# A hybrid decoder layer on one core: token blocks of 256, 512, 256 with the middle one dense, and its first expert products queued through the last block

## The chip, the core and the metric

The kernel runs on one core of a Trainium2 chip. The metric is the device time of one execution in microseconds (us); lower is better. The engines are PE (TensorE matmul, with PEld for its weight loads), DVE (VectorE), ACT (ScalarE), POOL (GpSimd) and SP (SyncE, which issues most DMAs). Each engine works through its own queue in a fixed order.

## What is computed

One decoder layer over 1024 tokens of width 1024, in float32.

```python
h = rms_norm(x, ln_mix)
z, xbc, dt, u, v, q, gates = split(h @ w_in)              # 8720 columns
y_ssd  = ssd_branch(xbc, z, dt, ...)                      # conv 4, scan in chunks of 128, state carried on
y_gmlp = gmlp_branch(u, v, ...)                           # 128x128 causal mixing in each chunk
y_mem  = memory_cross_attention(q, rms_norm(mem), w_mem_kv)   # 4 heads of 256
merged = sum_n sigmoid(gates_n) * (branch_n @ w_branch_n)
x = x + merged @ w_out
x = x + peer_ffn(rms_norm(x, ln_ffn), ...)
out = rms_norm(x, ln_final)

def peer_ffn(xt):                       # per token: 8 heads, 16 of 16384 experts each
    sc = (xt @ w_peer_q) . keys         # 2 x 128 scores a head, top 16 of each, then 16 of the pairs
    act = gelu(u[eid] . xt);  return sum(softmax(best) * act * v[eid])
```

Order in time is bound by two things: the scan carries its state from block to block, and the experts of a token are known only once the mixer and the routing of its block are through.

## The kernel before

The tokens are cut into the blocks of `BLOCKS`, here 0-255, 256-511 and 512-1023. For each block `mixer` runs as a generator: convolution tiles (`conv_tile`), the scan in chunks of 128 (`chunk_a`, `chunk_b`), the z and v projections (`tok`), three branches (`branch`) and the output projection. `routing` finds the 128 experts of each token of a block; most of its work is small DVE instructions (maxima, indices, one-hots). The main loop weaves routing of a block with the convolution tiles of the next one (`beside`), and with part of its sigmoid gates, which are spilled to DRAM (`spill`).

Every product with weights goes through `unit`: SP loads 512 KB, ACT rounds them to a high part (L159), POOL or DVE subtracts to get a low part (L160; DVE takes a share `lo_dve`), and PE does three products a tile (`mm3`, L186 to L188): 24 matmuls a unit, as wide as the block has tokens. `tok` uses the weights as the moving operand, 512 wide.

The experts are computed in two ways. For 512 tokens they are **gathered**: `gathered` takes four tiles of 128 tokens; for each there are 128 rows of `u` and 128 of `v`, each row an indirect DMA of 512 KB issued by POOL (L798) and one DVE instruction (L808 for `u`, L815 for `v`). That is 1024 gathered rows in all. A tile can begin when its block is routed. `pace` ties a row to a unit of the dense stage or, early on, to a unit of the second block; rows between `n1` and `NPRE` are tied to none (`n` counts pairs of rows). For the other 512 tokens they are **dense**: `dense` computes all 128x128 experts. For each of 128 first indices `dense_act` makes a unit of 24 matmuls, 512 wide, and a Gelu (an "act" below); `weigh` multiplies it by the gates and splits it; then come 128 units of `v`. The gates come from a matrix that `gate_matrix` builds in the "gates" stage, 16 stages of 8 steps (L832 to L844), and sends to DRAM (`g_d`).

Before, the dense tokens are the last block. While it is routed, 32 acts (`ACT_SPILL` = 4 a head) are computed beside it and spilled to `act_d`; 8 more (`AHEAD`) follow, and the other 88 are made in the dense stage.

Buffers that matter: `a16` (pool `actp`, four of 16 KB a partition), `b16` (pool `big`, two). The split normalized activations of 512 tokens (`xnT`) take two `a16`. Before, the routing of the last block also lives in an `a16` (`routing(xnT, a16(), ...)`), of which `gate_matrix` reads the indices and gates, and `gate_matrix` stages its results in `a16` too.

Tile decides the order on each engine by priorities and a model of time when the program is built; the order is then fixed.

Of the kernel before, what the change touches and what calls it, by code (L numbers as in the profile page):

```python
# [8 lines left out]
F32 = mybir.dt.float32  # L9
F32R = mybir.dt.float32r  # L10
# [13 lines left out]
BLOCKS = ((0, 256), (256, 256), (512, 512))  # L24
# [17 lines left out]
NG = 8  # L42
POOL_G = 3
NPRE = 270
LAG = 2
RATE_ROUTING, RATE_MIXER = 0.25, 0.36
ACT_SPILL = 4
# [11 lines left out]
def layer_kernel(ctx, tc, a, out_d):  # L59
# [59 lines left out]
    iota4 = const.tile([P, P, 4], BF16, name="iota4")  # L119
    nc.gpsimd.iota(iota4, pattern=[[1, P], [0, 4]], base=0, channel_multiplier=0,  # L120
# [15 lines left out]
    NSP = ACT_SPILL * HEADS  # L136
# [74 lines left out]
    def act_tiles(n=T):  # L211
        if n <= T // 2:
            t = a16(F32R)
            return tuple(t[:, j * KD * n:(j + 1) * KD * n].rearrange("p (k t) -> p k t", k=KD) for j in range(2))
        return (a16(F32R).rearrange("p (k t) -> p k t", k=KD), a16(F32R).rearrange("p (k t) -> p k t", k=KD))
# [106 lines left out]
    def mixer(b, hT, lmt=None):  # L322
# [8 lines left out]
        xy = b16()[:, :TT * D].rearrange("p (c d) -> p c d", c=TT)  # L331
# [4 lines left out]
        bc = a16()  # L336
        bcT = bc[:, 0:4 * T].rearrange("p (f t) -> p f t", f=4)
        btok = bc[:, 2048:2048 + TT * 256].rearrange("p (c n) -> p c n", c=TT)
        nsm = [0]

        def s64():
            o = 3072 + 64 * nsm[0]
            nsm[0] += 1
            return bc[:, o:o + NS].rearrange("p (c h) -> p c h", c=TT)
# [152 lines left out]
        vg = b16()[:, :TT * D].rearrange("p (t d) -> p t d", t=TT)  # L497
# [29 lines left out]
        yT = act_tiles(T)  # L527
# [34 lines left out]
        kv = b16()  # L562
# [3 lines left out]
        yT = act_tiles(T)  # L566
# [51 lines left out]
        for h in range(1, H_XA):  # L618
            qs = query(h)
            pTs = turn_probs(prs)  # L620
            prs = attend(h, qs)
            values(h - 1, pTs)
        pTs = turn_probs(prs)
        values(H_XA - 1, pTs)
        yield "attended"
        x2 = b16()[:, :TT * D].rearrange("p (t d) -> p t d", t=TT)
# [3 lines left out]

        mT = act_tiles(T)
# [14 lines left out]
        if t0 + T == SEQ:  # L646
# [13 lines left out]
        for t in range(TT):  # L660
            nc.sync.dma_start(xn_d[t0 + t * P:t0 + (t + 1) * P, :], x2[:, t, :])
            transposed(xnT, x2[:, t, :], t)
# [3 lines left out]
    def routing(xnT, rt, gt=None, eid=None, beside=lambda: None):  # L666
# [5 lines left out]
        ij = [rt[:, 2 * U + n * T:2 * U + (n + 1) * T].rearrange("p (t s) -> p t s", t=TT) for n in range(2)]  # L672
        if gt is None:
            gt = rt[:, 3 * U:3 * U + T].rearrange("p (t s) -> p t s", t=TT)
# [3 lines left out]
        for h in range(HEADS):  # L678
# [61 lines left out]
            for i in range(2):  # L740
                o1 = ohb[:, i * U:(i + 1) * U]
                o2 = ohb[:, (2 + i) * U:(3 + i) * U]
                nc.vector.tensor_tensor(o1.rearrange("p (a r c) -> p a r c", a=16, c=4),
                                        ab[:, i, :].rearrange("p (r c) -> p r c", c=4)[:, None].to_broadcast([P, 16, NK // 4, 4]),
                                        iota4[:, 0:16, None, :].to_broadcast([P, 16, NK // 4, 4]), op=ALU.is_equal)
                nc.gpsimd.tensor_tensor(o2.rearrange("p (a t k) -> p a t k", a=16, t=TT),
                                        o1.rearrange("p (a t k) -> p a t k", a=16, t=TT),
                                        topi[:, :, i, :].rearrange("p t a -> p a t")[:, :, :, None].to_broadcast([P, 16, TT, 16]),
                                        op=ALU.mult)
                nc.vector.tensor_reduce(ij[i][:, :, h * 16:(h + 1) * 16],  # L750
                                        o2.rearrange("p (a t k) -> p t k a", a=16, t=TT), axis=AX.X, op=ALU.add)
# [14 lines left out]
        return ij[0], ij[1], gt  # L766

    def final_rows(tt, acc):
        rs = slice(tt * P, (tt + 1) * P)
# [18 lines left out]
    def gathered(tt, eid, gt, pace):  # L788
        rs = slice(tt * P, (tt + 1) * P)
# [14 lines left out]
        xn = held(xn_d[rs, :])  # L804
# [7 lines left out]
        acc = held(x2_d[rs, :])  # L812
# [6 lines left out]
    def gate_matrix(t, i_f, j_f, gt, dp):  # L819
        tp = tp_ps()  # L820
        for n, v in enumerate((j_f, gt, i_f)):
            nc.tensor.transpose(tp[:, n * P:(n + 1) * P], v, ident)
        tr = sml.tile([P, P], F32, tag="tr", name="tr", bufs=2)
        nc.scalar.copy(tr, tp[:, P:2 * P])
        for s in range(P // STG):
# [20 lines left out]
            nc.sync.dma_start(g_d[t * (P // STG) + s], stage.rearrange("p i t -> p (i t)"))  # L846

# [87 lines left out]
    gate = gat.tile([P, TT, SLOTS], F32, tag="gate", name="gate", bufs=1)  # L935

    def until(m, label):
        while next(m) != label:
            pass

# [4 lines left out]
    for b in range(1, len(BLOCKS)):  # L945
# [10 lines left out]
        xnT = next(now)  # L956

# [8 lines left out]
        def beside():  # L966
            until(nxt, "conv")
            spill(GATE_SPILL)

        ts = slice(2 * b - 2, 2 * b)  # L970
        rate[0] = RATE_ROUTING if b == 1 else 0
        shared.append(b16())
        routing(xnT, shared[0][:, 0:2048], gate[:, ts], eid[:, ts], beside=beside)
        lo_dve[0] = 0 if b == 1 else LO_MIXER
        rate[0] = RATE_MIXER if b == 1 else 0
# [5 lines left out]
    until(now, "attended")  # L981
    until(now, "normed")
    xnT = next(now)
    spilled = {AHEAD + (n * (NI - AHEAD)) // NSP: n for n in range(NSP)}
    todo = [(i, n) for i, n in spilled.items()]
    stg = b16().rearrange("p (n t) -> p n t", n=8)

    def beside():
        for _ in range(ACT_SPILL):
            i, n = todo.pop(0)  # L990
            nc.sync.dma_start(act_d[n], dense_act(i, xnT, None, stg[:, n % 8], mm_ps()))

    lo_dve[0] = 0
    r = routing(xnT, a16(), beside=beside)
# [3 lines left out]
    acts = [dense_act(i, xnT, dp) for i in range(AHEAD)]  # L998
    for t in range(TT):
        gate_matrix(t, r[0][:, t], r[1][:, t], r[2][:, t], dp)  # L1000
    m_dense = len(marks)
    lo_dve[0] = LO_DENSE
    dense(SEQ // 2, xnT, dp, acts)
# [86 lines left out]
```

## Time and profile before

| what | value |
|---|---|
| median of 3 runs | 3732.34 us (3722.38 to 3734.37) |
| profiled execution | 3742.35 us, span 3740.6 us |
| busy share of the span | PE 89%, DVE 78%, POOL 68%, ACT 39% |
| mean granted clock of TensorE | 0.943 of full |
| DMA | 1012.82 MB, mean 271 GB/s |

The shares are means over stages with different limits, so they say little by themselves. The span is read in eight stretches, cut at places of the PE queue: 0-471 memory keys and first block; 471-725 routing of the first block beside the start of the second, up to its scan; 725-1043 the rest of the second block; 1043-1422 its routing beside the start of the third; 1422-1887 the rest of the third; 1887-2275 its routing, with 32 acts; 2275-2500 gates; 2500-3741 dense.

### The profile page before, as it was taken

The page shows a single profiled execution, that of the slowest core. Times are in us where ns is not written, and L with a number is a line of the kernel's source. Part 1 is how long each engine was busy: PE and PEld are TensorE (multiplying, and loading weights), DVE is VectorE, ACT ScalarE, POOL GpSimd, SP SyncE. Part 2 cuts the span into 40 slices and gives each one's busy share as a digit, 9 for nine tenths or more (in the row PEclk, how much of TensorE's full clock was granted, in tenths as well). Part 3 has the DMA queues.
Part 4 walks back from the last instruction along what each step waited for, and adds up shares of the span by engine and source line. Part 5 has one row for each costly group of instructions (what it writes and reads, how often), then busy time and mean ns, then how long its engine had stood idle before and what let it go on. Part 6 is the DMA issues. An engine that isn't in the chain of part 4 may idle for free. (4 is left out here: it accounts for less than half of the span.)

```text
span 3740.6 us, 49425 instructions
## 1 busy us (share of the span) xinstructions
PE 3312.7 (89%) x16928; PEld 2792.3 (75%) x16928; DVE 2918.0 (78%) x5380; ACT 1454.8 (39%) x2192; POOL 2533.8 (68%) x1867
## 2 busy tenths in 40 slices
PE   7999977888878879999898777779999999999998
PEld 6799877777767757777676656668878888888776
DVE  2532588653699999878899997778788888888888
ACT  4554555543444533323232324763222223222222
POOL 6577767787777777786877565446666666666664
PEclk9999988988989989999999997889999999999999
DMA  5245555576797779999988663369999999999996
GB/s 190 102 165 185 206 175 180 172 248 236 279 328 263 267 243 349 352 363 340 338 312 270 216 212 141 155 257 319 331 330 338 336 348 337 345 346 348 328 329 255
DMA packets 353437, 1012.82 MB, mean 271 GB/s; under 512 B 32545, under 2 KB 117921, under 8 KB 350753
## 3 DMA queue, kind: packets, MB, share of 16 engines
q0 software_dynamic: 147456, 536.94, 39.3%
q1 hardware_dynamic: 205728, 472.72, 36.3%
q8 instruction: 134, 2.20, 0.2%
q14 instruction: 119, 0.97, 0.1%
HBM read 945.56 MB, written 63.96 MB: 270 GB/s over the span
## 5 line engine op out<-in xcount | busy, mean ns | idle before, releaser
L160 POOL TENSOR_TENSOR wlo<-raw,whi 128x1024 fp32r<-128x1024 f32 x491 | 1178.2, 2403 | 480.1 <-ACT whi L159 358.8
L159 ACT CAST whi<-raw 128x1024 fp32r<-128x1024 f32 (+1 forms) x623 | 648.1, 1045 | 1183.7 <-issue 419.6
L186 PE MATMUL mm_ps<-a,whi 128*128 128x256 f32 (+2 forms) x2552 | 865.3, 343 | 73.8 <-ACT t L320 15.4
L188 PE MATMUL mm_ps<-a,wlo 128*128 128x256 f32 (+2 forms) x2552 | 862.1, 340 | 50.6 <-POOL wlo L160 48.5
L187 PE MATMUL mm_ps<-a,whi 128*128 128x256 f32 (+2 forms) x2552 | 861.2, 338 | 6.8 <-DVE a L160 4.3
L798 POOL DMA_INDIRECT g<-in_v_dram,eid x512 | 527.3, 1030 | 291.1 <-DVE row_ps L815 101.4
L808 DVE SCALAR_TENSOR_TENSOR g<-g,row_ps 128x1024 f32<-128x1024 f32 x512 | 607.7, 1213 | 120.9 <-DMA g<-in_u_dram,eid 116.5
L798 POOL DMA_INDIRECT g<-in_u_dram,eid x512 | 528.9, 1033 | 208.1 <-DVE g L808 92.9
L815 DVE SCALAR_TENSOR_TENSOR row_ps<-g,dots,row_ps 128x1024 f32<-128x1024 f32 x512 | 656.3, 1282 | 8.0 <-ACT row_ps L785 1.2
L186 PEld LDWEIGHTS mm_ps<-a,whi 128*128 128x128 f32 (+1 forms) x2552 | 509.4, 201 | 127.8 <-issue 21.6
L188 PEld LDWEIGHTS mm_ps<-a,wlo 128*128 128x128 f32 (+1 forms) x2552 | 508.4, 200 | 105.5 <-POOL wlo L160 61.4
L187 PEld LDWEIGHTS mm_ps<-a,whi 128*128 128x128 f32 (+1 forms) x2552 | 510.8, 200 | 50.6 <-DVE a L160 5.1
L186 PE MATMUL mm_ps<-whi,d 128*128 128x512 f32 x1024 | 385.5, 398 | 28.2 <-ACT d L159 21.0
L187 PE MATMUL mm_ps<-wlo,d 128*128 128x512 f32 x1024 | 407.5, 398 | 1.0 <-DVE wlo L160 0.8
L188 PE MATMUL mm_ps<-whi,d 128*128 128x512 f32 x1024 | 403.8, 396 | 0.0
L188 PE MATMUL tp_ps<-a,wlo 128*128 128x512 f32 x768 | 304.4, 396 | 11.4 <-POOL wlo L160 10.8
L186 PE MATMUL tp_ps<-a,whi 128*128 128x512 f32 x768 | 304.3, 396 | 11.3 <-ACT d L930 9.5
L187 PE MATMUL tp_ps<-a,whi 128*128 128x512 f32 x768 | 303.9, 396 | 0.0
L186 PEld LDWEIGHTS mm_ps<-whi,d 128*128 128x128 f32 x1024 | 193.8, 189 | 77.4 <-ACT d L159 21.4
L160 DVE TENSOR_TENSOR wlo<-raw,whi 128x1024 fp32r<-128x1024 f32 x132 | 179.1, 1357 | 91.8 <-ACT whi L159 91.8
L187 PEld LDWEIGHTS mm_ps<-wlo,d 128*128 128x128 f32 x1024 | 193.9, 189 | 47.5 <-DVE wlo L160 1.1
L188 PEld LDWEIGHTS mm_ps<-whi,d 128*128 128x128 f32 x1024 | 193.4, 189 | 45.5
(257 smaller groups left out, 4985.0 us busy)
## 6 DMA issues: line engine op xcount, KB each, us to landing
raw<-in_win_a_dram SPq DMA_DIRECT2D x156, 512.0 KB, 4.3
raw<-in_uT_a_dram SPq DMA_DIRECT2D x128, 512.0 KB, 5.5
raw<-in_v_b_dram SPq DMA_DIRECT2D x128, 512.0 KB, 6.7
raw<-in_br_a_dram SPq DMA_DIRECT2D x72, 512.0 KB, 4.3
g_d<-a SPq DMA_DIRECT2D x16, 2048.0 KB, 6.3
a<-g_d SPq DMA_DIRECT2D x32, 1024.0 KB, 10.9
raw<-in_win_b_dram SPq DMA_DIRECT2D x48, 512.0 KB, 4.2
raw<-in_pq_a_dram SPq DMA_DIRECT2D x48, 512.0 KB, 4.7
```

The costliest lines, as they stand in the source:

```text
L159: return (nc.scalar.copy(hi, src), (eng or nc.vector).tensor_tensor(lo, src, hi.bitcast(F32), op=ALU.subtract))
L160: (eng or nc.vector).tensor_tensor(lo, src, hi.bitcast(F32), op=ALU.subtract))
L186: nc.tensor.matmul(ps, lhsT=l_hi, rhs=r_hi, start=start, stop=False)
L187: nc.tensor.matmul(ps, lhsT=l_hi, rhs=r_lo, start=False, stop=False)
L188: nc.tensor.matmul(ps, lhsT=l_lo, rhs=r_hi, start=False, stop=stop)
L798: nc.gpsimd.indirect_dma_start(out=g, out_offset=None, in_=a[table], in_offset=bass.IndirectOffsetOnAxis(ap=eid[:, k:k + 1], axis=0))
L808: nc.vector.scalar_tensor_tensor(g, g, 1.0, xn, op0=ALU.mult, op1=ALU.mult, accum_out=col(w, k))
L815: nc.vector.scalar_tensor_tensor(acc, g, col(w, k), acc, op0=ALU.mult, op1=ALU.add)
```

## The change

The blocks become 0-255, 256-767 and 768-1023, and block `DENSE` = 1, the middle one, is the dense one. The gathered tiles are then tokens 0-255 and 768-1023 (`ROW0`). The routing results of the dense block go to tiles of their own (`ij_dense`, `gate_dense`), and its `xnT` is held to the end (`held_xT`). `fill` computes acts and spills them to `act_d`, 64 in all: 3 a head while the middle block is routed beside the start of the last one (24), 2 after each of its two chunks (4), 2 at each of ten new `yield "gap"` places in the rest of its mixer (20), 2 a head in the routing of the last block (16). Eight more are woven into `gate_matrix`, one after every second stage, and the dense stage makes 56. The last block is "packed" (`compact`): its working tiles share one `b16`, and two of its transposed operands use `b16` for `a16`. `NG`, the number of gather buffers, goes from 8 to 7, `NPRE` from 270 to 300, and the rate for early rows from 0.25 and 0.36 (routing, mixer) to 0.5 (routing only). The DVE share of low parts, `LO_MIXER`, now applies from the end of the first routing to the end of the second, so to the middle block.

```diff
-BLOCKS = ((0, 256), (256, 256), (512, 512))
+BLOCKS = ((0, 256), (256, 512), (768, 256))
+DENSE = 1
+ROW0 = (0, 128, 768, 896)
...
-NG = 8
+NG = 7
-NPRE = 270
+NPRE = 300
-RATE_ROUTING, RATE_MIXER = 0.25, 0.36
-ACT_SPILL = 4
+RATE_ROUTING = 0.5
+ACT_SPILL = 64
+FILL_ROUTING = (3, 2)
+FILL_GAP = 2
...
-        xy = b16()[:, :TT * D].rearrange("p (c d) -> p c d", c=TT)
+        compact = b == len(BLOCKS) - 1
+        main = b16()
+        xy = main[:, :TT * D].rearrange("p (c d) -> p c d", c=TT)
...
-        bc = a16()
+        bc = main[:, 2048:] if compact else a16()
...
         for j in range(2):
+            yield "gap"
             pss = tok(a["win_b"][FB_Z + j], hT)
...
-        merged = b16()[:, :KD * T].rearrange("p (k t) -> p k t", k=KD)
+        merged = (main if compact else b16())[:, :KD * T].rearrange("p (k t) -> p k t", k=KD)
...
-        yT = act_tiles(T)
+        yield "gap"
+        yT = act_tiles(T, b16 if compact else a16)
...
-        kv = b16()
+        kv = a16() if compact else b16()
...
         for h in range(1, H_XA):
+            yield "gap"
             qs = query(h)
...
-    def gate_matrix(t, i_f, j_f, gt, dp):
+    def gate_matrix(t, ij, gt, dp, beside):
...
             nc.sync.dma_start(g_d[t * (P // STG) + s], stage.rearrange("p i t -> p (i t)"))
+            beside(t * (P // STG) + s)
...
+    def fill(count, dp=None):
+        for _ in range(count):
+            if todo:
+                i, n = todo.pop(0)
+                act = d2(dp) if dp else tmp.tile([P, T], F32, tag="sp", name="sp", bufs=2)
+                nc.sync.dma_start(act_d[n], dense_act(i, held_xT[0], None, act, mm_ps()))
...
         def beside():
             until(nxt, "conv")
             spill(GATE_SPILL)
+            if held_xT:
+                fill(FILL_ROUTING[0])
...
-        lo_dve[0] = 0 if b == 1 else LO_MIXER
-        rate[0] = RATE_MIXER if b == 1 else 0
+        lo_dve[0] = LO_MIXER if b == 1 else 0
+        rate[0] = 0
...
-    r = routing(xnT, a16(), beside=beside)
+    for label in now:
+        if label == "gap":
+            fill(FILL_GAP)
+        elif not isinstance(label, str):
+            xnT = label
+    routing(xnT, b16()[:, 0:2048], gate[:, 2:4], eid[:, 2:4], beside=lambda: fill(FILL_ROUTING[1]))
...
-    acts = [dense_act(i, xnT, dp) for i in range(AHEAD)]
+    def beside_gates(n):
+        fill(left * (n + 1) // 16 - left * n // 16, dp)
+        if n % 2:
+            acts.append(dense_act(len(acts), held_xT[0], dp, None, mm_ps()))
```

The queue of PE shows what stands at the `gap` places. In the cross-attention of a block of 256 tokens, before (the second block; L584 scores, L613 values, L186 to L188 a unit on the block's own activations a_4385, 256 wide):

```order
L584 MATMUL mm_ps<-b_8605,t_8817 128x256
L584 MATMUL mm_ps<-b_8605,t_8850 128x256
L613 MATMUL mm_ps<-t_8858,b_8605 128x256 x2
L186 MATMUL mm_ps<-a_4385,whi 128x256
L187 MATMUL mm_ps<-a_4385,whi 128x256
L188 MATMUL mm_ps<-a_4385,wlo 128x256
```

The same place of the last block now (L623 values; a_10387 and a_10388 are the high and low part of the dense block's `xnT`):

```order
L623 MATMUL mm_ps<-t_16333,a_15944 128x256
L623 MATMUL mm_ps<-t_16335,a_15944 128x256
L190 MATMUL mm_ps<-a_10387,whi 128x512
L191 MATMUL mm_ps<-a_10388,whi 128x512
L192 MATMUL mm_ps<-a_10387,wlo 128x512
```

An act of the dense block, 512 wide, stands where the next unit of the block itself stood.

The queue of DVE in the routing of the dense block, before (L699 to L722 maxima and indices, L815 `v` rows of the second gathered tile):

```order
L699 MAX topv<-t_16092 128x8 x4
L815 SCALAR_TENSOR_TENSOR row_ps<-g_29237,dots,row_ps 128x1024
L722 MAX_INDEX bp<-a_15290,c_15801 128x8
L720 MATCH_REPLACE c_15813<-a_15290 128x112
L700 MAX_INDEX ti<-topv,t_16092 128x8 x4
L815 SCALAR_TENSOR_TENSOR row_ps<-g_29240,dots,row_ps 128x1024
L720 MATCH_REPLACE c_15819<-a_15290 128x112
L721 MAX a_15290<-c_15813 128x8
```

The same routing now (L821 `u` rows of the second gathered tile, L307 convolution of the last block, L164 low part of a unit):

```order
L821 SCALAR_TENSOR_TENSOR g_28965,dots<-g_28965,row_ps 128x1024
L307 SCALAR_TENSOR_TENSOR t_11164<-mm_ps,pk,t_11164 128x254
L821 SCALAR_TENSOR_TENSOR g_28968,dots<-g_28968,row_ps 128x1024
L718 MAX_INDEX ti<-topv,s_10979 128x8
L724 TENSOR_TENSOR b_10445<-topv 128x48
L718 MAX_INDEX ti<-topv,s_10985 128x8
L724 TENSOR_TENSOR b_10445<-topv 128x48
L373 TENSOR_TENSOR b_10218<-b_10218 128x32
L821 SCALAR_TENSOR_TENSOR g_28971,dots<-g_28971,row_ps 128x1024
L164 TENSOR_TENSOR wlo<-raw,whi 128x1024
```

The routing of 512 tokens now shares DVE with the start of a mixer and with low parts, besides the gathered rows. Counted in the DVE queue, the gathered rows of the eight stretches, in the order of the table of stretches above, were 0, 27, 62, 134, 216, 104, 7 and 474, and are now 0, 104, 208, 169, 31, 64, 31 and 417.

## Rows read from the trace of the kernel before

**Rows 1.** The page: busy us of each engine, and PE and DVE in 40 slices.

```profile
PE 3312.7 (89%) x16928; PEld 2792.3 (75%) x16928; DVE 2918.0 (78%) x5380; ACT 1454.8 (39%) x2192; POOL 2533.8 (68%) x1867
PE   7999977888878879999898777779999999999998
DVE  2532588653699999878899997778788888888888
```

**Rows 2.** Windows, eight stretches: length, busy us (x instructions), granted clock, DMA share, GB/s.

```profile
0.00:471.00 471.00, 419.99 (x2901) 388.00 (x2902) 174.58 (x312) 250.28 (x414) 331.62 (x171) 0.96 0.49 170
471.00:725.00 254.00, 199.75 (x1418) 191.16 (x1416) 203.86 (x737) 138.59 (x214) 175.89 (x119) 0.87 0.51 174
725.00:1043.00 318.00, 257.96 (x1522) 225.68 (x1521) 178.59 (x276) 130.45 (x203) 245.49 (x162) 0.90 0.73 254
1043.00:1422.00 379.00, 316.32 (x1607) 261.17 (x1608) 375.85 (x870) 160.42 (x252) 282.90 (x228) 0.90 0.80 276
1422.00:1887.00 465.00, 426.59 (x1844) 341.58 (x1844) 389.10 (x519) 148.69 (x230) 354.30 (x285) 0.95 0.94 348
1887.00:2275.00 388.00, 322.12 (x1366) 257.31 (x1366) 386.23 (x1136) 118.23 (x154) 255.52 (x184) 0.94 0.68 234
2275.00:2500.00 225.00, 174.51 (x1145) 158.55 (x1143) 168.45 (x277) 160.88 (x268) 123.81 (x142) 0.88 0.47 189
2500.00:3741.00 1241.00, 1195.50 (x5136) 968.85 (x5136) 1041.34 (x1259) 347.23 (x458) 764.27 (x581) 0.98 0.91 329
```

**Rows 3.** Windows of the gathered tile g alone: DVE, POOL, clock, DMA share, GB/s.

```profile
471.00:725.00 254.00, 32.83 (x54) 28.29 (x29) 0.87 0.51 174
725.00:1043.00 318.00, 72.27 (x119) 62.93 (x65) 0.90 0.73 254
1043.00:1422.00 379.00, 170.99 (x179) 133.88 (x136) 0.90 0.80 276
1422.00:1887.00 465.00, 256.29 (x339) 217.97 (x212) 0.95 0.94 348
1887.00:2275.00 388.00, 134.36 (x136) 97.14 (x100) 0.94 0.68 234
2275.00:2500.00 225.00, 10.77 (x18) 8.68 (x9) 0.88 0.47 189
2500.00:3741.00 1241.00, 589.17 (x694) 507.26 (x475) 0.98 0.91 329
```

**Rows 4.** Windows of 100 us: first projections (256 wide), two of gates, dense (512 wide).

```profile
200.00:300.00 100.00, 98.80 (x791) 96.74 (x790) 29.42 (x43) 54.25 (x81) 86.47 (x48) 1.00 0.58 196
2300.00:2400.00 100.00, 64.91 (x419) 63.14 (x419) 72.71 (x120) 65.15 (x107) 45.61 (x56) 0.77 0.31 132
2400.00:2500.00 100.00, 92.78 (x655) 81.61 (x654) 84.36 (x139) 89.47 (x151) 59.31 (x71) 0.99 0.55 224
2800.00:2900.00 100.00, 100.00 (x434) 81.38 (x434) 88.59 (x87) 28.30 (x36) 63.49 (x50) 1.00 0.92 336
```

**Rows 5.** Groups of instructions: count, then busy us and mean ns, then idle before.

```profile
L160 DVE TENSOR_TENSOR wlo<-raw,whi 128x1024 fp32r<-128x1024 f32 x132 | 179.1, 1357 | 91.8 <-ACT whi L159 91.8
L320 ACT ACT_TABLE_LOAD x41 | 52.6, 1283 | 0.7
```

**Rows 6.** Waits of 2275 to 2409 (total, times, longest), and the ACT timeline there.

```profile
PE mm_ps L842 <- issue: 27.0, 5, 6.8
ACT a L844 <- DMA g_d<-a: 12.7, 6, 3.8
...
2350.51 1.87 ACT L844 COPY a<-mm_ps 128x512 f32<-128x512 f32 x2 [1.77 <-DMA g_d<-a]
```

**Rows 7.** Waits of 725 to 1043: total us, times, longest us.

```profile
ACT whi L159 <- PE mm_ps L187: 58.5, 21, 11.9
...
DVE t L516 <- DMA t<-gate_d: 12.2, 2, 8.0
...
PEld tp_ps L284 <- DVE b L495: 7.3, 1, 7.3
```

More of the change, by code (lines that the diff above doesn't have):

```diff
@@ L209, in tok, with act_tiles @@
         return pss
[L211 removed]
+    def act_tiles(n=T, of=a16):
         if n <= T // 2:
[L213 removed]
+            t = of(F32R)
             return tuple(t[:, j * KD * n:(j + 1) * KD * n].rearrange("p (k t) -> p k t", k=KD) for j in range(2))
@@ L565, in mixer @@
         vm = kv[:, 2048:4096].rearrange("p (t d) -> p t d", t=2)
-        yT = act_tiles(T)
+        yT = act_tiles(T, b16 if compact else a16)
         def query(h):
@@ L660, in mixer, with routing @@
         for t in range(TT):
-            nc.sync.dma_start(xn_d[t0 + t * P:t0 + (t + 1) * P, :], x2[:, t, :])
+            n = ROW0.index(t0) + t
+            nc.sync.dma_start(xn_d[n * P:(n + 1) * P, :], x2[:, t, :])
             transposed(xnT, x2[:, t, :], t)
         yield xnT
-    def routing(xnT, rt, gt=None, eid=None, beside=lambda: None):
+    def routing(xnT, rt, gt, eid=None, ij=None, beside=lambda: None):
         T = xnT[0].shape[-1]
@@ L749, in routing @@
                                         op=ALU.mult)
-                nc.vector.tensor_reduce(ij[i][:, :, h * 16:(h + 1) * 16],
-                                        o2.rearrange("p (a t k) -> p t k a", a=16, t=TT), axis=AX.X, op=ALU.add)
+                with nc.allow_low_precision(reason="one of the 16 is an integer below 128, the others are 0"):
+                    nc.vector.tensor_reduce(ij[i][:, :, h * 16:(h + 1) * 16],
+                                            o2.rearrange("p (a t k) -> p t k a", a=16, t=TT), axis=AX.X, op=ALU.add)
             beside()
@@ L816, in gathered @@
         final_rows(tt, acc)
-    def gate_matrix(t, i_f, j_f, gt, dp):
+    def gate_matrix(t, ij, gt, dp, beside):
         tp = tp_ps()
-        for n, v in enumerate((j_f, gt, i_f)):
+        wide = d2(dp).rearrange("p (n s) -> p n s", n=4)
+        nc.vector.tensor_copy(wide[:, 0:2, :], ij[:, :, t, :])
+        for n, v in enumerate((wide[:, 1, :], gt[:, t, :], wide[:, 0, :])):
             nc.tensor.transpose(tp[:, n * P:(n + 1) * P], v, ident)
@@ L939, in until @@
             pass
+    spilled = {AHEAD + (n * (NI - AHEAD)) // NSP: n for n in range(NSP)}
+    todo = [(i, n) for i, n in spilled.items()]
+    held_xT = []
+    def fill(count, dp=None):
[4 more added lines that the diff above has]
+                nc.sync.dma_start(act_d[n], dense_act(i, held_xT[0], None, act, mm_ps()))
     mT = mem_norm()
@@ L956, in layer_kernel @@
         xnT = next(now)
+        if b - 1 == DENSE:
+            held_xT.append(xnT)
         def spill(count):
@@ L968, in beside @@
             spill(GATE_SPILL)
-        ts = slice(2 * b - 2, 2 * b)
+            if held_xT:
+                fill(FILL_ROUTING[0])
         rate[0] = RATE_ROUTING if b == 1 else 0
         shared.append(b16())
-        routing(xnT, shared[0][:, 0:2048], gate[:, ts], eid[:, ts], beside=beside)
-        lo_dve[0] = 0 if b == 1 else LO_MIXER
-        rate[0] = RATE_MIXER if b == 1 else 0
+        if b - 1 == DENSE:
+            routing(xnT, shared[0], gate_dense, ij=[ij_dense[:, n] for n in range(2)], beside=beside)
+        else:
+            routing(xnT, shared[0][:, 0:2048], gate[:, 0:2], eid[:, 0:2], beside=beside)
+        lo_dve[0] = LO_MIXER if b == 1 else 0
+        rate[0] = 0
         now = nxt
@@ L980, in layer_kernel @@
             spill(KD // chunks)
[L981 to L993, printed above, removed]
-    r = routing(xnT, a16(), beside=beside)
+            if held_xT:
+                fill(FILL_GAP)
+    for label in now:
+        if label == "gap":
+            fill(FILL_GAP)
+        elif not isinstance(label, str):
+            xnT = label
+    routing(xnT, b16()[:, 0:2048], gate[:, 2:4], eid[:, 2:4], beside=lambda: fill(FILL_ROUTING[1]))
     mix.close()
@@ L997, in layer_kernel @@
     dp = ctx.enter_context(tc.tile_pool(name="dp", bufs=1, reuse_waits="tile"))
-    acts = [dense_act(i, xnT, dp) for i in range(AHEAD)]
+    acts = []
+    left = len(todo)
+    def beside_gates(n):
+        fill(left * (n + 1) // 16 - left * n // 16, dp)
+        if n % 2:
+            acts.append(dense_act(len(acts), held_xT[0], dp, None, mm_ps()))
     for t in range(TT):
-        gate_matrix(t, r[0][:, t], r[1][:, t], r[2][:, t], dp)
+        gate_matrix(t, ij_dense, gate_dense, dp, beside_gates)
     m_dense = len(marks)
     lo_dve[0] = LO_DENSE
-    dense(SEQ // 2, xnT, dp, acts)
+    dense(BLOCKS[DENSE][0], held_xT[0], dp, acts)
     m_last = len(marks)
```

36 lines of the change are left out of this document (20 added, 16 removed).

## The prediction

> **What bounds the kernel now.** The page's shares come first [rows 1]: PE is busy 89% of the span and DVE 78%, and the slices show that they take turns. In the first four slices DVE has two to five tenths while PE has seven to nine; in the middle DVE stands at nine; in the last third PE does. So no single share tells what a change is worth, and the span is taken stretch by stretch [rows 2]. What the reader should look for there is which engine fills its stretch:
>
> - 1043-1422 (routing of 256 tokens beside the start of a 512 block): DVE 375.85 of 379, 99%. 1887-2275 (routing of 512): DVE 386.23 of 388. These two end with DVE, whatever PE does.
> - 1422-1887 (rest of the 512 block): PE 426.59 of 465, DVE 389.10, DMA share 0.94: all near their end.
> - 725-1043 (rest of a 256 block): PE 257.96 of 318, DVE 178.59. Nothing is full; PE and ACT wait for each other in turn (58.5 us of ACT's waits are for the matmuls) [rows 7]. Here PE has 60 us free.
> - 2275-2500 (gates): nothing is full either. In the first half the granted clock is 0.77 and 419 matmuls pass in 100 us, in the second 0.99 and 655 [rows 4]; ACT waits there for the staged result to leave for DRAM, and PE stands behind it up to 6.8 us at a time [rows 6]. The code says why: of four `a16`, two hold `xnT` and one the routing results until the last tile has been read, so that one buffer is left for staging.
> - 2500-3741 (dense): PE, 434 matmuls of 512 columns in 100 us, 0.230 us each [rows 4], with the DMA share at 0.91 and DVE at 84% [rows 2].
>
> **What the change moves.** The work is the same: as many units, as many gathered rows. What moves is (a) 32 acts out of the dense stage, (b) acts into the PE gaps of a 256 block, (c) the gathered rows, and (d) the place of the two routings. Prices: an act is 24 x 0.230 = 5.5 us of PE [rows 4]. A gathered row is 1.237 us of DVE: the DVE times of the gathered tile add up to 1266.7 us [rows 3] over 1024 rows. The rows of each stretch now are those counted in the DVE queue.
>
> The first block keeps its 471 us; four convolution tiles of the next block that fall into it are 512 wide: 4 x 24 x (0.230 - 0.126) = 10 us, with 0.126 from 791 matmuls in 100 us [rows 4]. **481**.
>
> Routing of the first block beside the start of the 512 block. It is the old stretch 1043-1422 with 104 rows. DVE without rows was 376 - 171 = 205 [rows 2, 3]; 205 + 104 x 1.237 = 334, at 99% **337** (PE's 316 busy would allow it).
>
> Rest of the 512 block: as 1422-1887, with 208 rows for 212. **465**.
>
> Routing of 512 beside the start of the last block. No such stretch exists; DVE is summed. Routing of 512: 386 - 134 = 252 [rows 2, 3]. The start of a 256 block: 204 - 33 = 171 less the routing of 256 in it. That routing lies between half of 252 (126) and the whole 171; I take 140, near the half, since the instructions are the same and half as many or half as wide. 171 - 140 = 31. Gathered rows 169 x 1.237 = 209. Twenty low parts on DVE at 1.357 [rows 5]: 27. Together 519, at 99% **524** (510 to 538 by the ends). PE's 28 acts here cost nothing: with about 200 us of the block's own start [rows 2], 88 of query projections (16 x 5.5) and 154 of acts PE has 442, under DVE's 524. If DVE were not full, PE would be next.
>
> Rest of the last block: old 725-1043 plus 20 acts, 110 us of PE. If all of it fits into waits, 318; if none does, 428. PE had 60 us free in that stretch [rows 2], so 50 are left over: 368, less a little for 31 rows instead of 65: **365**.
>
> Routing of the last block with 16 acts: DVE 140 + 64 x 1.237 = 219, **221** (207 to 252 by the ends of the routing); PE has 88 + 16 x 24 x 0.126 = 136 and is hidden.
>
> Gates: the routing results no longer sit in an `a16`, so two buffers stage from the start. By the second half's speed, 655 matmuls in 100 us, the 1024 take 156 us; by the old time 225. DVE sets a floor: 168 - 11 + 31 x 1.237 = 195 [rows 2, 3]. **200**, near the floor; eight acts on PE (44 us) fit under it.
>
> Dense: 32 acts fewer, 1241 - 32 x 5.5 = 1064. DVE: 1041 - 589 + 417 x 1.237 - 16 low parts x 1.357 = 946, 89% of that. DMA: 329 GB/s x 1241 us = 408 MB, less 32 units and 58 rows of 0.524 MB, plus 32 acts of 0.262 MB to read back: 369 MB; at the 348 GB/s of 1422-1887 [rows 2] that is 1061 us, at the 329 of this stretch 1122. All three limits come close, so I add a little: **1070**.
>
> Sum: 481 + 337 + 465 + 524 + 365 + 221 + 200 + 1070 = 3663, against the span of 3741: 78 less. The profiled execution took 3742.35 with 1.75 outside the span; the median of the runs is 10 below it. 3732 - 78 = 3654, so **3655**. Where it comes from: dense -171, gates -25 and the last routing -167 (256 tokens now, not 512, with 64 rows for 104), against +275 in the stretches between 471 and 1887, which were 1416 and become 1691, and +10 in the first block. The acts save time in dense only because DVE, not PE, ends the stretches that take most of them.
>
> **A rule that speaks against it.** ACT now loads tables 25 times instead of 9 in the rest of the 256 block, counted in its queue, since each Gelu stands between other functions. A load is 1.283 us [rows 5]: 16 more are 21 us, on an engine that had 188 of 318 us free there [rows 2], so nothing is added to the 365. The Trainium skill, ScalarE: Activation LUTs, section "What ACT_TABLE_LOAD costs", gives the same 1283 ns and about 1380 ns of drain on top, 2.66 us for each switch; an estimate by it is 43 us, and the sum 3663 would be 3706 if every switch lay on the path. No drain has a row of its own here.
>
> **The rivals.**
>
> All acts hidden. The rest of the last block stays at 318, the gates at DVE's 195 and the dense stage at 1061: 3663 - 47 - 5 - 9 = 3602, or 3592 as a median. For it: 60 us of idle PE, and a granted clock of 0.90 there that can rise [rows 2]. Against: a queue is in order, so an act that starts before a short chain ends holds the chain up to 5.5 us.
>
> The dense stage ends with the transfers. If 0.91 busy at 329 GB/s is all this mixture gives, dense takes 1122: 3663 + 52 = 3715, median 3706. For it: the spilled acts, twice as many, and fewer gather buffers (7). Against: 348 GB/s at 0.94 in 1422-1887.
>
> No act hidden. 428 in the rest of the last block, and the table loads on the path: +63 + 21 = 3747, median 3738, within 0.3% of before (0.3%, about what a measurement of this kernel can tell from no change, is 11 us).
>
> Slower: the packed block stands in line for buffers. Two `a16` hold the dense `xnT`, one the block's own input, so the scan's scratch, the first transposed operand, `kv` and the last two operands follow one another through one `a16` and one `b16`. Each of five hand-overs can show a wait like the 7.3 us before the transposes or the 8.0 us for a gate tile [rows 7], some 15 us together, on top of acts that hide nothing: 428 + 75 = 503, +138, median 3792. It decides from the point where that stretch exceeds 365 + 88 = 453. Against: the second block had the same hand-overs with more buffers, and its waits of this kind were short.
>
> **How the numbers follow.** Forecast 0.50 (its own range 3615 to 3700), all hidden 0.14, transfers 0.14, nothing hidden 0.12, buffers 0.10. The range 3590 to 3745 holds all but the slower rival and half of the first: a little over 8 in 10. Faster by over 0.3% (below 3721): the forecast but for 0.04 of its upper tail, the first, and most of the second: 0.73. Within 0.3%: nearly all of the third and a part of that tail: 0.13. Slower (above 3743): the last rival and the rest of the tails: 0.14.
>
> **What would show it.** Right: a stretch of some 520 us in the middle with DVE at 99%, while the old one of 388 before the gates is gone; the rest of the last block near 365 with PE above 90%; gates without PE standing behind the staged result; a dense stage of about 1070 with PE full. Wrong: DVE below 95% in the second routing (then acts hold up chains); the last block beyond 453; a dense stage in which PE waits for `wlo`, for acts from DRAM or for weighing.

## The result: slower by 1.3%

The changed kernel took 3776.79 us (median of 4 runs, 3768.97 to 3782.7) against 3727.36 for the kernel before; the ratio is 1.0133, with a 95% interval of 1.0101 to 1.0166. The forecast was 3655, faster. The profiled execution has a span of 3767.2 us.

The windows of the changed kernel, in eight stretches cut at the same places of the queues as those of [rows 2] (length, busy us and instructions of PE, PEld, DVE, ACT, POOL, granted clock, DMA share, GB/s):

```profile
0.00:478.00 478.00, 425.40 (x2906) 390.50 (x2906) 178.13 (x311) 254.37 (x414) 330.08 (x171) 0.98 0.52 169
478.00:841.00 363.00, 313.27 (x1607) 260.85 (x1608) 326.06 (x924) 156.32 (x248) 258.15 (x201) 0.92 0.71 244
841.00:1308.00 467.00, 438.44 (x1966) 354.40 (x1966) 397.15 (x494) 162.18 (x258) 351.97 (x279) 0.96 0.94 344
1308.00:1825.00 517.00, 394.88 (x2102) 339.11 (x2100) 503.23 (x1342) 211.15 (x286) 357.40 (x268) 0.87 0.80 273
1825.00:2165.00 340.00, 321.80 (x1861) 280.28 (x1861) 134.49 (x156) 155.88 (x225) 248.78 (x141) 0.98 0.65 219
2165.00:2390.00 225.00, 157.18 (x852) 135.82 (x850) 210.88 (x696) 76.58 (x110) 157.56 (x126) 0.87 0.75 254
2390.00:2653.00 263.00, 196.47 (x1207) 176.38 (x1208) 204.46 (x346) 166.97 (x275) 150.87 (x169) 0.82 0.52 201
2653.00:3767.00 1114.00, 1045.04 (x4439) 836.99 (x4437) 956.01 (x1128) 302.43 (x400) 672.73 (x508) 0.97 0.94 335
```

| stretch | forecast | measured | off |
|---|---|---|---|
| first block | 481 | 478 | -3 |
| first routing, start of the 512 block | 337 | 363 | +26 |
| rest of the 512 block | 465 | 467 | +2 |
| routing of 512, start of the last block | 524 | 517 | -7 |
| rest of the last block | 365 | 340 | -25 |
| last routing | 221 | 225 | +4 |
| gates | 200 | 263 | +63 |
| dense | 1070 | 1114 | +44 |
| sum | 3663 | 3767 | +104 |

Two steps failed, the gates and the dense stage; the rest of the last block and the second routing were right only in their sums, as the experiments show. At the entry of the gates PE stood still. The PE timeline, the waits of 2365 to 2653 (total, times, longest), and the windows of 20 us before the gates and 40 us from their start:

```profile
2400.95 0.45 PE L837 MATMUL tp_ps<-ident,d 128*128 128x128 f32 x1 [32.23 <-DVE d L835]
```

```profile
POOL d L851 <- DVE d L847: 40.6, 56, 9.7
PE mm_ps L857 <- POOL d L851: 39.4, 17, 6.9
...
PE tp_ps L837 <- DVE d L835: 32.2, 1, 32.2
```

```profile
2380.00:2400.00 20.00, 0.00 (x0) 0.00 (x0) 19.93 (x48) 0.23 (x1) 14.03 (x14) 0.50 0.82 266
2400.00:2440.00 40.00, 19.80 (x76) 16.78 (x77) 39.78 (x70) 12.57 (x20) 27.01 (x30) 0.50 0.93 336
```

The first transposes of the gates wait 32 us for a copy on DVE (L835), which is full (19.93 of 20) with the end of the routing and with `u` rows of the third gathered tile. The granted clock is at half until 2440, and DVE is full all that time. At the other end, the windows from the last matmul to the end and the gathered tile in the last stretches (there: DVE, POOL, clock, DMA):

```profile
3729.00:3767.00 38.00, 0.55 (x3) 0.11 (x1) 32.34 (x39) 4.25 (x9) 12.91 (x13) 0.57 0.70 259
```

```profile
1825.00:2165.00 340.00, 39.80 (x31) 26.84 (x27) 0.98 0.65 219
2165.00:2390.00 225.00, 67.73 (x111) 59.59 (x62) 0.87 0.75 254
2390.00:2653.00 263.00, 46.32 (x80) 31.59 (x33) 0.82 0.52 201
```

Behind the last matmul DVE works for another 32 us at rows and final scaling. In the kernel before, the last row ended 2 us after the last matmul.

### The profile page after: what moved, and what is told of

It reads as the page before. It is cut to its first block, busy times and chain, and to the rows that moved or that the text cites. A ratio compares the mean times of both kernels' runs of the same rounds, so it can differ in the third digit from the quotient of the medians.

```text
span 3767.2 us, 49553 instructions
## 1 busy us (share of the span) xinstructions
PE 3292.5 (87%) x16928; PEld 2774.3 (74%) x16928; DVE 2910.4 (77%) x5391; ACT 1485.9 (39%) x2212; POOL 2527.5 (67%) x1860
## 4 chain that ended last, share of the span: by engine, by line
PE 35%; DVE 22%; issue 8%; POOL 5%; ACT 3%; DMA 2%; POOLq 0%; DVEq 0%; ACTq 0%; SPq 0%
PE mm_ps L191 9%; PE mm_ps L192 9%; PE mm_ps L190 9%; DVE g L821 5%; DVE row_ps L828 3%; POOL g L811 2%; PE tp_ps L192 2%; PE tp_ps L190 2%; PE tp_ps L191 2%; POOL wlo L164 2%; PE mm_ps L857 1%; DVE d L847 1%; DVE wlo L164 1%; DMA g<-in_v_dram,eid 1%; ACT a L859 1%
## 5 line engine op out<-in xcount | busy, mean ns | idle before, releaser
L164 POOL TENSOR_TENSOR wlo<-raw,whi 128x1024 fp32r<-128x1024 f32 x484 | 1162.1, 2404 | 423.9 <-ACT whi L163 396.8
L190 PE MATMUL mm_ps<-a,whi 128*128 128x512 f32 (+1 forms) x2744 | 947.6, 349 | 113.6 <-ACT whi L163 42.9
L192 PE MATMUL mm_ps<-a,wlo 128*128 128x256 f32 (+1 forms) x2744 | 937.3, 344 | 33.1 <-DVE wlo L164 19.6
L191 PE MATMUL mm_ps<-a,whi 128*128 128x512 f32 (+1 forms) x2744 | 941.2, 343 | 1.1 <-DVE a L164 0.9
L811 POOL DMA_INDIRECT g<-in_v_dram,eid x512 | 537.8, 1050 | 361.8 <-DVE row_ps L828 212.2
L190 PEld LDWEIGHTS mm_ps<-a,whi 128*128 128x128 f32 x2744 | 534.2, 195 | 182.6 <-ACT whi L163 49.6
L821 DVE SCALAR_TENSOR_TENSOR g<-g,row_ps 128x1024 f32<-128x1024 f32 x512 | 608.5, 1208 | 40.5 <-DMA g<-in_u_dram,eid 40.2
L192 PEld LDWEIGHTS mm_ps<-a,wlo 128*128 128x128 f32 x2744 | 533.2, 195 | 94.8 <-DVE wlo L164 21.6
L191 PEld LDWEIGHTS mm_ps<-a,whi 128*128 128x128 f32 x2744 | 535.4, 195 | 56.6 <-DVE a L164 2.1
L164 DVE TENSOR_TENSOR wlo<-raw,whi 128x1024 fp32r<-128x1024 f32 x139 | 194.6, 1400 | 58.0 <-ACT whi L163 57.0
L857 PE MATMUL mm_ps<-d,d 128*128 128x128 f32 x1024 | 156.6, 315 | 55.6 <-POOL d L851 39.4
L857 PEld LDWEIGHTS mm_ps<-d,d 128*128 128x128 f32 x1024 | 143.8, 223 | 69.0 <-POOL d L851 54.9
L847 DVE TENSOR_TENSOR d<-iota,tp_ps 128x512 bf16<-128x512 f32 (+1 forms) x256 | 155.5, 678 | 36.9 <-ACT tr L839 24.8
```

Source lines behind the costliest of these rows:

```text
L164: (eng or nc.vector).tensor_tensor(lo, src, hi.bitcast(F32), op=ALU.subtract))
L190: nc.tensor.matmul(ps, lhsT=l_hi, rhs=r_hi, start=start, stop=False)
L191: nc.tensor.matmul(ps, lhsT=l_hi, rhs=r_lo, start=False, stop=False)
L192: nc.tensor.matmul(ps, lhsT=l_lo, rhs=r_hi, start=False, stop=stop)
L811: nc.gpsimd.indirect_dma_start(out=g, out_offset=None, in_=a[table], in_offset=bass.IndirectOffsetOnAxis(ap=eid[:, k:k + 1], axis=0))
L821: nc.vector.scalar_tensor_tensor(g, g, 1.0, xn, op0=ALU.mult, op1=ALU.mult, accum_out=col(w, k))
```

## The experiments

In these, stretches are cut at PE's matmuls alone: the second routing from its first key product to the end of the scan (511 us in the changed kernel), the rest of the last block to the next key product (353), last routing and gates to the last gate product (474), dense to the end (1115).

**Rows of the third tile moved.** First all of them out of the stretches before the dense stage:

```diff
-NPRE = 300
+NPRE = 256
```

> NPRE 256 for 300: no row of the third gathered tile before the dense stage is free of a unit, so the 62 rows that stood in the last routing and most of the 31 in the gates go to the dense stage. Theory A (those rows stand ahead of the end of the routing and of the gates on DVE, and PE waits for it): the routing and the gates, 485 us in the changed kernel (2165 to 2650), shrink by 60 to 90, to some 400 to 425, and the wait of the gate transposes for DVE (32 us) is gone. Theory B (the gates are long because acts are woven into them): they stay within 20 us of 485. The dense stage gets 86 rows of 1.24 us more on an engine that had 160 us free: if DVE ends it, it grows by up to 107 from 1117; if it has room, by less than 40. Whole: A 3750 to 3800, B 3800 to 3880.

Measured: 3794.24 us, ratio to before 1.0179 (1.0144 to 1.0213). Last routing and gates fell from 474 to 373, by more than A's 60 to 90, and PE's wait at the entry is 9.5 us instead of 32.2. The dense stage grew from 1115 to 1230. Windows of last routing and gates, of dense to the last matmul, and of what follows:

```profile
2189.00:2562.00 373.00, 321.70 (x1976) 286.74 (x1975) 302.67 (x863) 235.79 (x375) 221.39 (x207) 0.92 0.44 166
2562.00:3641.00 1079.00, 1046.84 (x4438) 836.22 (x4437) 921.45 (x1177) 299.53 (x390) 656.53 (x497) 0.99 0.94 338
3641.00:3792.00 151.00, 0.82 (x4) 0.34 (x2) 141.88 (x124) 4.25 (x9) 91.51 (x97) 0.51 0.92 358
```

PE was through 1079 us into the dense stage and the rows ran on for another 142. The 86 rows saved 101 us in one place and cost 115 in the other.

Then the same rows kept before the dense stage, but tied to the eight acts of the gates:

```diff
+        if n < 2 * SLOTS:
+            return None
         if n < NPRE:
-            return None
+            return marks[m_gates + int((n - 2 * SLOTS) * (m_dense - m_gates) / (NPRE - 2 * SLOTS))]
```

> The same 88 rows of the third tile before the dense stage, but each tied to one of the eight acts in the gates, so that 12 instead of 64 stand in the last routing and 83 instead of 31 in the gates. Theory A (rows ahead of the routing's end are what costs): routing and gates shrink from 485 by 30 to 60, the dense stage stays at 1117, whole 3710 to 3745. Theory B (woven acts are the cost) and theory C (the sum of DVE's work from the last routing to the end is what counts, wherever a row stands): 485 stays within 15, whole 3760 to 3790.

Measured: 3793.92, ratio 1.0175 (1.014 to 1.021). PE entered the gates 60 us earlier, and the gates took 330 instead of 248; both together rose from 474 to 495. Theory A fell: in the gates these rows cost no less than in the routing. The window of last routing and gates:

```profile
2179.00:2674.00 495.00, 342.76 (x1973) 306.73 (x1972) 402.09 (x1035) 243.28 (x374) 303.11 (x292) 0.81 0.59 215
```

**No rows at all behind the last block.**

```diff
-    for t in range(TT):
+    for t in range(2):
         gathered(t, eid[:, t], gate[:, t], pace)
```

> The third and fourth gathered tile are left out (512 of 1024 rows; the last 256 tokens get no output), so nothing gathered stands on DVE after the rest of the last block. Theory A (rows on DVE are what makes the last stretches long): last routing and gates together 340 to 400 us instead of 485, and the dense stage 1035 to 1065 instead of 1117, with PE at 98% or more. Theory B (woven acts): routing and gates above 450. Everything before 2165 stays as in the changed kernel.

Measured: 3599.56 (one time). Last routing and gates, and dense:

```profile
2180.00:2536.00 356.00, 315.65 (x1971) 280.30 (x1970) 292.68 (x845) 233.40 (x374) 212.36 (x197) 0.96 0.43 159
2536.00:3598.00 1062.00, 1034.04 (x4443) 834.96 (x4442) 466.69 (x534) 298.70 (x387) 219.29 (x91) 0.99 0.45 143
```

356 us without rows, with DVE busy 293 only. The changed kernel has 95 rows there and takes 474: (474 - 356) / 95 = 1.24 us a row, the whole DVE time of a row, though DVE is not full. The run with 9 rows gives 101 / 86 = 1.17. PE's own dense stage is 1062, 13 of it behind the last matmul; the forecast had 1064 for it.

**The weave.** The eight acts ahead of the gates instead of between their stages:

```diff
-    acts = []
+    acts = [dense_act(n, held_xT[0], dp, None, mm_ps()) for n in range(AHEAD)]
...
-        if n % 2:
-            acts.append(dense_act(len(acts), held_xT[0], dp, None, mm_ps()))
```

> The eight acts woven into the gates are made ahead of them, as in the kernel before. Without any rows the gates took 208 us with the woven acts, 198 in the kernel before. Theory A (the woven acts cost nothing, rows add in full): last routing and gates together stay within 15 of 474. Theory B (the weave stretches the gates): they fall by 20 to 45.

Measured: 3749.93 (one time). Theory B: 447 for 474, though five rows more fall into it. The window:

```profile
2188.00:2635.00 447.00, 355.04 (x2021) 302.83 (x2020) 421.72 (x1046) 239.46 (x377) 314.46 (x299) 0.90 0.68 247
```

**What holds the dense stage.** Low parts from DVE to POOL:

```diff
-LO_MIXER, LO_DENSE = 0.34, 0.5
+LO_MIXER, LO_DENSE = 0.34, 0.3
```

> LO_DENSE 0.3 for 0.5: some 37 of 92 low parts of the dense stage go from DVE (1.4 us each) to POOL (2.4 us each). In the changed kernel the last gathered rows ran 28 us on DVE after the last matmul. Theory A (the dense stage ends with DVE): 37 x 1.4 = 52 us of DVE less, the end of the rows moves up by 25 to 45, whole 3735 to 3755. Theory B (gathers are bound by transfers or by their seven buffers): within 10 us of 3777, and POOL's longer splits may delay the issue of rows and make it slower, up to 3800.

Measured: 3789.89, ratio 1.0159 (1.0124 to 1.0193); the stage took 1140. This shows little of DVE: 36 low parts left it, but it was busy for 944 us after 956, since other instructions took longer, while POOL had 751 for 673. That POOL's work made the stage longer fits, and is not shown by itself.

DVE's additions left out (ACT copies the results out instead):

```diff
-                    nc.vector.tensor_tensor(dst, dst, pss[t], op=ALU.add)
+                    nc.scalar.copy(d2(dp), pss[t])
```

> In the dense stage DVE no longer adds the 176 results to the sum (0.68 us each, 120 us in all); ACT, 27% busy, copies them out of PSUM instead, so that units, rows, transfers and POOL's work stay. The dense tokens get no expert sum. Theory A (DVE ends the dense stage, as it never gets beyond 86% there): the stage falls from 1115 to 1062 to 1080 and the last row ends before the last matmul. Theory B (transfers or POOL's row issues set it): it stays above 1100.

The gate matrix read twice instead of 32 times:

```diff
-            if g < NI // GCH:
+            if g < 2:
```

> The dense stage reads the gate matrix only twice instead of 32 times (30 of some 374 MB of that stage; later products use old gates, so the dense tokens are not what they should be); units, rows, DVE, POOL and PE work stay. Theory A (the stage ends with the transfers, DMA share 0.94 at 335 GB/s): 8% fewer bytes, the stage falls from 1115 towards PE's 1062, to 1060 to 1080, the last row ends with the last matmul. Theory B (the rows' order on POOL and DVE against seven buffers): it stays at 1100 or more.

Measured: 3761.84 and 3751.95 (one time each). The dense windows of the changed kernel, without the additions, and with two reads:

```profile
2652.00:3767.00 1115.00, 1046.04 (x4445) 837.76 (x4443) 956.01 (x1128) 303.43 (x401) 672.73 (x508) 0.97 0.94 335
```

```profile
2658.00:3760.00 1102.00, 1041.67 (x4442) 833.51 (x4442) 841.68 (x952) 398.98 (x576) 672.96 (x508) 0.98 0.94 339
```

```profile
2666.00:3749.00 1083.00, 1041.42 (x4444) 839.19 (x4443) 954.43 (x1128) 304.61 (x401) 670.67 (x508) 0.98 0.86 316
```

114 us less on DVE shortened the stage by 13 (theory B), with the DMA share still at 0.94. 8% fewer bytes, with DVE as before, shortened it by 32, to just above A's range, and the last row then ended 3 us before the last matmul. So transfers hold this stage, more than DVE does. The waits say by which way; in the changed kernel, and then with two reads (total, times, longest):

```profile
POOL g L811 <- DVE row_ps L828: 178.8, 150, 7.8
...
ACT whi L163 <- DMA raw<-in_v_b_dram: 64.9, 17, 11.1
...
DVE d L898 <- ACT d L946: 52.5, 25, 5.3
...
DVE g L821 <- DMA g<-in_u_dram,eid: 9.1, 3, 4.9
```

```profile
POOL g L811 <- DVE row_ps L828: 23.7, 23, 3.0
...
DVE d L898 <- ACT d L946: 7.4, 5, 3.3
```

In the changed kernel DVE waits only 10 us in all for gathered rows: the rows do not land late. But the units of `v` come late, ACT waits 65 us for them, DVE's queue waits 52 us for ACT's Gelu, and POOL waits for DVE to free a gather buffer. With two reads ACT has no wait for units of `v` left in its list. A few of the 21 us that are left to 1062 may be DVE's, and an eighth gather buffer may have helped too; no run separates them.

**The acts before the dense stage.** Nearly none queued early:

```diff
-ACT_SPILL = 64
-FILL_ROUTING = (3, 2)
-FILL_GAP = 2
+ACT_SPILL = 1
+FILL_ROUTING = (0, 1)
+FILL_GAP = 0
```

> Only one act is queued ahead of the dense stage, in the last routing, so 63 move into it: 63 x 5.5 = 345 us of PE there. Theory A (the queued acts are hidden in the second routing, half hidden in the rest of the last block and hidden in the last routing; the dense stage with that much PE work hides all its rows): second routing unchanged at 511, rest of the last block 353 to about 320, last routing unchanged, dense 1062 + 345 = 1407; whole about 4020. Theory B (acts hold up the chains they are queued in): the stretches before the gates lose 100 us or more, whole below 3950.

Measured: 3913.76 (one time), theory B. The second routing took 488 instead of 511, the rest of the last block 260 (with 15 rows) instead of 353 (with 31), the dense stage 1392. The rows that left the rest of the block went to the second routing, which had 187 for 171, with DVE busy for 486 of its 488 us. With 16 rows of 1.237 us less it would be some 468, so the 28 acts there cost about 43 us, 1.5 each (an estimate; no run changes them alone). The rest of the last block without acts, and with them:

```profile
1812.00:2072.00 260.00, 228.42 (x1466) 203.68 (x1466) 113.12 (x147) 115.57 (x181) 190.99 (x109) 0.95 0.62 208
```

```profile
1825.00:2178.00 353.00, 332.85 (x1944) 290.30 (x1944) 138.37 (x161) 162.88 (x235) 253.37 (x143) 0.99 0.65 221
```

The block's own work and 15 rows need 260, not the 318 that the old stretch suggested. With twenty acts and 31 rows it is 353. Waits of that stretch with acts (total, times, longest), and the same two softmax waits with the same 31 rows but without acts (the version with 44 acts, below), show how:

```profile
DVE t L615 <- PE tp_ps L611: 37.7, 4, 14.2
DVE b L164 <- ACT b L163: 26.7, 5, 17.8
...
DVE mx L597 <- PE mm_ps L594: 18.4, 4, 12.3
```

```profile
DVE mx L597 <- PE mm_ps L594: 15.3, 4, 9.9
...
DVE t L615 <- PE tp_ps L611: 9.8, 3, 4.5
```

The copies of the softmax transposes (L615) wait up to 14.2 us, 38 us in all for 10 without acts, for matmuls that PE takes only after the acts in front of them. The softmax's own wait (L597) is nearly as long without acts.

The kernel before without its 32 acts:

```diff
-        for _ in range(ACT_SPILL):
+        for _ in range(0):
             i, n = todo.pop(0)
...
-    spilled = {AHEAD + (n * (NI - AHEAD)) // NSP: n for n in range(NSP)}
+    spilled = {}
```

> The kernel before without its 32 acts in the last routing; they are made in the dense stage. Theory A (they were hidden beside a routing of 512 tokens that DVE ends): the dense stage grows by 32 x 5.5 = 175 from 1244, the routing stays within 15 of 405, whole 3885 to 3900; so the acts queued early brought the old kernel some 165, more than the 137 that 63 brought the changed one (3914 without, 3777 with). Theory B (they were half in the way): the routing shrinks by 50 or more, whole below 3850.

Measured: 3840.6 (one time), theory B: the routing took 353 instead of 405, the dense stage 1399 instead of 1244. So 32 early acts brought the old kernel 3841 - 3733 = 108 us, 3.4 us each, and 63 bring the changed one 3914 - 3777 = 137, 2.2 each (the runs without acts are one time each).

**Rows moved into the rest of the last block**, where DVE is 40% busy:

```diff
+        if n < 185:
+            return None
+        if n < 2 * SLOTS:
+            return marks[m_rest + int((n - 185) * (m_r2 - m_rest) / (2 * SLOTS - 185))]
         if n < NPRE:
             return None
```

> The rows from pair 185 on (142 rows of the first two tiles) are tied to units in the rest of the last block, where DVE had 206 of 340 us free; 107 rows leave the second routing, whose stretch ended with DVE (509 us busy of 525). Theory A (DVE's rows set that stretch, and in the rest of the block they cost nothing): the second routing's stretch, 511 us by the keys' and the scan's matmuls, shrinks by 80 to 130 until PE (403 us busy) is next, the rest of the last block (353) grows by less than 30, whole 3670 to 3720. Theory B (rows cost their 1.24 us wherever they stand in the queue): the rest grows by what the routing loses, whole 3750 to 3790.

Measured: 3768.36, ratio 1.0104 (1.0083 to 1.0126). The second routing fell from 511 to 417, as A says; the rest of the last block rose from 353 to 426, against A, and the whole is in B's range. 109 rows gave 94 us in one place (0.86 each) and cost 73 in the other (0.67 each); the other stretches took most of the difference. The two windows:

```profile
1323.00:1740.00 417.00, 376.08 (x2078) 326.25 (x2077) 363.32 (x1208) 203.49 (x279) 248.31 (x156) 0.94 0.60 200
1740.00:2166.00 426.00, 356.05 (x1942) 305.43 (x1941) 264.71 (x285) 161.74 (x233) 354.28 (x252) 0.94 0.88 315
```

**A version put together from this.** The acts of the `gap` places and the weave taken back (44 acts queued early), and then also fewer early rows:

```diff
-ACT_SPILL = 64
+ACT_SPILL = 44
...
         if label == "gap":
-            fill(FILL_GAP)
+            fill(0)
...
-    acts = []
+    acts = [dense_act(n, held_xT[0], dp, None, mm_ps()) for n in range(AHEAD)]
...
-        if n % 2:
-            acts.append(dense_act(len(acts), held_xT[0], dp, None, mm_ps()))
```

> The changed kernel with the twenty acts in the rest of the last block left to the dense stage (44 queued early for 64) and the eight acts ahead of the gates, not woven in. Theory A (an act in the rest of the last block costs 4.6 of its 5.5 us there, and one in the dense stage is free as long as the rows, not PE, end it): rest of the last block 353 to about 260, gates and last routing 474 to about 447, dense 1115 to 1170 to 1190; whole 3700 to 3735. Theory B (the dense stage pays each act in full on top of what it has): dense 1225, whole about 3770.

```diff
-NPRE = 300
+NPRE = 268
```

> As the kernel with 44 early acts, and NPRE 268 for 300, so that 63 rows more go from the last routing and the gates to the dense stage. Theory A (a row costs 1.24 us before the dense stage, and nothing in it until transfers or rows end it): last routing and gates fall by a further 70 to 80, the dense stage grows by 0 to 40; whole 3650 to 3700, below the kernel before. Theory B (the dense stage is already at its limit of rows, 0.374 a us): it grows by 63 / 0.374 = 168 from 1115, whole 3730 or more.

Measured: 3725.26, ratio to before 0.9985 (0.9972 to 0.9998), and 3718.9, ratio 0.9964 (0.9951 to 0.9976). The first came out by theory A: 269 in the rest of the last block, 452 in last routing and gates, 1168 in dense. The second lies between its theories: it gave 60 us more before the dense stage and lost 57 in it. Rest of the last block, last routing and gates, dense, of the first and then of the second:

```profile
1830.00:2099.00 269.00, 230.07 (x1472) 203.60 (x1472) 143.03 (x161) 116.81 (x183) 205.48 (x124) 0.96 0.67 232
2099.00:2551.00 452.00, 357.00 (x2016) 303.84 (x2014) 425.37 (x1044) 241.06 (x379) 313.14 (x297) 0.89 0.67 243
2551.00:3719.00 1168.00, 1131.28 (x4872) 916.88 (x4872) 958.83 (x1129) 332.89 (x436) 671.88 (x513) 0.99 0.90 322
```

```profile
1833.00:2102.00 269.00, 229.47 (x1468) 201.23 (x1466) 139.59 (x161) 115.93 (x182) 205.41 (x124) 0.97 0.67 230
2102.00:2494.00 392.00, 344.12 (x2013) 296.44 (x2012) 341.06 (x918) 238.21 (x379) 251.23 (x234) 0.94 0.53 196
2494.00:3719.00 1225.00, 1134.91 (x4872) 917.13 (x4872) 1040.33 (x1255) 333.84 (x437) 750.18 (x576) 0.96 0.93 334
```

With the same 31 rows, twenty acts fewer make the rest of the last block 353 - 269 = 84 us shorter, 4.2 of the 5.5 us of each; the dense stage takes them for 53, since PE is at its end there (1172 by 1062 + 20 x 5.5) and the rows fit under it. Both versions are faster than the changed kernel, and the second is 0.36% faster than the kernel before.

## Why the prediction was wrong

**The stretches where DVE was full came out, one of them by luck.** The second routing was forecast at 524 from DVE's sum and took 517, with DVE at 503. But "PE's 28 acts here cost nothing" is not borne out: by the estimate above they cost some 43 us, 8 of them low parts on DVE that the sum held, so the rest of that sum was too large by about as much. Two slips beside it changed nothing: if the whole 171 is routing, the lower end is 488 / 0.99 = 493, not 510; and the 442 us of PE hold a routing of 256 tokens that is not in this stretch (PE was busy for 395). The rest of the 512 block was right to 2 us. In the first routing the sum of DVE was right (334 forecast, 326 measured) but not that it would be filled to 99%: 326 of 363 is 90%. With 104 rows for 134 the chains between DVE, ACT and PE show again; this reading was not tested by a run.

**Gates, +63: the step "DVE sets a floor, near the floor" failed.** It took the largest busy time for the length of a stretch in which no engine is full. Without rows the last routing and the gates take 356 with DVE at 293, and each row adds 1.24 us by that run, 1.17 by the first run above, with 9 rows, and 60 / 63 = 0.95 between the last two versions. So the two terms, 221 and 200, should have been 356 plus 95 rows, 474 by the cuts of the experiments. The weave cost 27 of the 474 (the run without it); what it costs without rows, in the 356, no run shows. The part of the step on the staging buffers is not borne out as a gain: the 156 us from the second half's speed were never reached, and the gates took 175 at best, with 8 rows and no weave. PE's waits behind the staged result before were real [rows 6], but other waits came in their place: for POOL's product, which waits for DVE (40.6 and 39.4 us).

**Dense, +44: the term "all three limits come close, so I add a little" was mis-sized.** PE's part was right (1064 forecast, 1062 without rows). Of the 53 us above that, 29 are in PE's own part (1077 to the last matmul, for 1048 without rows) and 24 behind it. The transfers, worked out as 1061 to 1122, were the end, and near the upper one: 335 GB/s at a share of 0.94, not 348; they came in by late units of `v`, which hold ACT and then DVE. That was the second rival's mechanism, and its 1122 is close to the 1114 measured. The forecast took the rate of 1422-1887 [rows 2], a stretch with other transfers; its 369 MB (57 rows less, not 58) were near the 373 moved.

**The rest of the last block, -25: two errors that cancel.** The idle 60 us of PE in 725-1043 [rows 2] were read as gaps that acts can fill. With 31 rows instead of 65 the stretch takes 269 without acts, not 318. The rows explain a part of that: here a row costs 0.67 us (109 moved in) or (269 - 260) / 16 = 0.56, so 34 rows are 19 to 23 of the 49 us, and the rest stays open. And an act costs 4.2 of its 5.5 us there: 269 + 84 = 353 (by these cuts), where I had 318 + 50. The sum was near; what it meant was not, since 20 acts that save 110 us in PE's dense stage cost 84 here, and then 53 of the stage's gain went to the transfers.

**The rivals.** The slower rival, the packed block standing in line for buffers, was not the cause: that block takes 260 to 269 without acts. The time came out on its side by two other mechanisms, each of which I had at hand: rows that cost up to their full time where nothing is full (my price of 1.237 us, not applied), and the transfers. The table loads of the rule named in the prediction stand in the stretch that was faster than forecast, 19 of them, against 7 without acts. A load there, in ACT's timeline:

```profile
2032.60 1.05 ACT L163 CAST whi<-raw 128x1024 fp32r<-128x1024 f32 x1 [1.12 <-issue]
2033.67 1.28 ACT L946 ACT_TABLE_LOAD   x1
2034.96 0.60 ACT L946 ACTIVATE sp<-mm_ps 128x512 f32<-128x512 f32 x1
```

From the end of the instruction before it to the start of the next it takes 1.31 us, the median of all 160 loads; the drain of about 1380 ns that the rule adds does not show. Twelve more are 16 us of ACT; which part of the 84 us for twenty acts they are, no run takes apart.

**The whole account.** Without early acts the two layouts are 73 us apart (3914 and 3841). The old one then gains 108 by 32 acts beside a routing of 512 tokens; the new one 137 by 63. That is 73 - 29 = 44 us slower by these single runs, against 49 by the medians. The 73 need not be the order of the blocks. Without early acts the new layout has 606 rows ahead of its dense stage and the old one 548, and both finish their rows under PE in a dense stage of 1392 and 1399 us. These 58 rows would be 72 us at 1.24 each and 32 at 0.56; no run has the new order with the old number.

## What to carry to other kernels

Where no engine is full, the length of a stretch is not the largest busy time: a chain passes through several in-order queues, and work put into one of them is best priced at its whole time until a run shows less (a row of 1.24 us cost from 0.56 to 1.24 here). Idle time of PE beside such a chain is not room for long work; two products of 5.5 us in a row held the transposes of a softmax up by as much as 14 us. When PE's work leaves a stage, count what else has to pass in it, transfers first, at the rate of that same mixture.

## What the runs showed of the hardware

With PE idle the granted clock in the records fell to 0.50 (2380 to 2440), so the first gate products after the wait ran at the lower of two levels. In the dense stage the transfers held at 335 to 339 GB/s with a share of 0.94, whether DVE had 956 or 842 us of work; with 8% fewer bytes the share fell to 0.86. Behind the last matmul of the run with `NPRE` 256, where little else moves, the gathered rows went at 358 GB/s with a share of 0.92, while DVE was busy for 142 of 151 us. A change of ACT's tables took 1.31 us from instruction to instruction.
